# A hybrid decoder layer on one core: rows of x, one block difference, one order edge, and the opening's queues and turns moved

## The chip, the cores and the metric

The kernel runs on one core of a Trainium2 chip. The core has a matrix engine (TensorE, called PE in the profile; PEld is its weight load), a vector engine (VectorE, DVE), a scalar engine (ScalarE, ACT), GpSimd (POOL) and a queue engine (SyncE, SP) that issues most transfers. The metric is the device time of one execution in microseconds (us).

## The reference

One layer of a decoder trunk, all in float32, on x of 1024 tokens by 1024 channels:

```
h = RMSNorm(x);  [q | k | v | u | g] = h @ W_in
branch A: differential attention (8 heads, QK norm, T5 bias, causal), RMS subln, @ W_proj_attn  -> y_a
branch B: GLU(u) -> causal depthwise conv, width 31 -> LayerNorm over channels -> swish, @ W_proj_conv -> y_b
m = sigmoid(g_a) * y_a + sigmoid(g_b) * y_b
x = x + m @ W_out
x = x + (silu(gate) * up) @ W_down,   [gate | up] = RMSNorm(x) @ W_gate_up
```

## The kernel before

Every float32 matrix product is made of three reduced-precision products: each operand is split into a high part (a cast on ACT, `split_hi`) and a low part (a subtraction on DVE, `split_lo`), and PE accumulates high x high, high x low and low x high. Where two 2 x 2 block products meet, seven block products are used in place of eight (u, w_out, gate and up, w_down), which needs sums and differences of blocks beforehand.

The program is traced into a planner, which gives every instruction a place on its engine by a simulated time line, the earlier traced one first among those that are ready; `after(ins)` adds an edge that keeps the instructions traced inside it behind `ins` on the engine of `ins`. `in_order()` does that for DVE, ACT and PE at once, and `steps(...)` calls functions one after the other in that way. Each engine then runs its list strictly in order.

Four places matter here.

*The opening.* x comes in tiles of 128 rows, `xts[i]`. The first, `xts[0]`, is loaded in two halves of 512 columns on SyncE's queue. The norm weights (`anw`, two loads on ACT's queue into one partition) are spread over all partitions by a product with ones (`spread_weights`) and copied into `wb`. `squares` and `roots` give each row's factor, `norm` applies factor and weights, `turn_x` transposes on PE into banks of a pool of two (`px`, the tile name in the profile) and casts the high part, `low_x` makes the low part and so frees the bank. `keep_busy` is filler on PE. `v_tile(i, first, n)` issues `n` of the 24 matmuls by which tile i enters the first block of v. `gemm_turn` is the second product of the first half of u: four of its eight slices k (three matmuls each), then `turn_low(5)`, then the other four; after it come `turn_low(6)`, `v_tile(4)`, `turn_low(7)`, `v_tile(5)`.

*LayerNorm.* After attention, `ln_both` interleaves the two token halves of the LayerNorm (`ln_chunks`); `ln_step` advances it by a listed number of pieces between the products of `w_proj_attn`. One piece takes differences from the mean on DVE (L1573) and squares on ACT. `ya_out` multiplies a product by its gate on DVE (L1642) and stores it; `gate_of[0, 0]` is the first of these multiplications, and an `after` keeps the third `ln_step`'s DVE instructions behind it.

*The product with w_out.* Seven block products in the order of `WSEVEN`: 11, 12, S1, S2, S4, S3, 22. Each has four steps j and four row tiles i, 48 matmuls. 11 goes into the banks b, 12 into four banks a, S1 and S4 into banks c, which are the same four PSUM buffers as a; S2, S3 and 22 into b. When a block product (or its second summand) is through, four additions on DVE (L1864) take the bank into the rows of x, `xa`, and thereby free it. `wload` loads a block of w_out, `sload` loads sums of m that were stored in the stage before, `x_rows(l, c)` loads 128-row tiles of x (four for each row half l, columns of half c), and `wless(z, a, b)` makes a block difference on DVE (L1779, four instructions). All are traced at the first product, z = 0, in a written order on SyncE; the tiles `xa` lie where the stage before had its buffers.

*Weights.* `ws.next()` hands out the next pair of high and low parts and splits up to two ahead, into buffers of three.

Of the kernel before, what the change touches and what calls it, by code (L numbers as in the profile page):

```python
# [10 lines left out]
F32 = mybir.dt.float32  # L11
F32R = mybir.dt.float32r
AF = mybir.ActivationFunctionType
ALU = mybir.AluOpType
AX = mybir.AxisListType

P = 128
S = 1024
D = 1024
# [13 lines left out]
NKT = D // P  # L33
# [24 lines left out]
def kernel(  # L58
# [27 lines left out]
    nc = tc.nc  # L86
    dve, act, pool, pe = nc.vector, nc.scalar, nc.gpsimd, nc.tensor
    PSUM = bass.MemoryType.PSUM

    xs = x[0]  # L90
# [31 lines left out]
    last_lo, last_mm = [None], [None]  # L122
# [12 lines left out]
    def after(ins):  # L135

        return nullcontext() if ins is None else tc.issue_after(ins)
# [41 lines left out]
    ap = a0.enter_context(tc.tile_pool(name="a0", bufs=2, reuse_waits="tile"))  # L179
# [6 lines left out]
    xts = {}  # L186
# [3 lines left out]
        queue.dma_start(xts[i][:], xs[i * P : (i + 1) * P, :])  # L190


    anw = [ap.tile([P, 512], F32R, tag="vh", name=f"anw{g}")[0:1, :].bitcast(F32) for g in range(2)]
    one = ap.tile([1, P], F32, name="one", bufs=1)
    busy = ap.tile([P, 512], F32R, tag="vl", name="busy")
    dve.memset(f32(busy[:]), 1.0)
    dve.memset(one[:], 1.0)
    for g in range(2):
        nc.scalar.dma_start(anw[g], attn_norm_w[:, 512 * g : 512 * (g + 1)])
    xts[0] = ap.tile([P, D], F32, tag="xt", name="xt0", bufs=4)  # L200
    for g in range(2):
        nc.sync.dma_start(xts[0][:, 512 * g : 512 * (g + 1)], xs[0:P, 512 * g : 512 * (g + 1)])
    wb = ap.tile([P, D], F32, name="anw_b", bufs=1)

    def keep_busy(n):

# [138 lines left out]
    class Stream:  # L345
# [12 lines left out]
        def next(self):  # L358
            self.fetch()
            return self.have.pop(0)  # L360
# [720 lines left out]
    def opening():  # L1081
# [16 lines left out]
        def v_tile(i, first=0, n=24):  # L1098

            if i % 2 == 0 and not first:  # L1100
                o[i // 2] = pg()
            ts, dst = slice(i * P, (i + 1) * P), o[i // 2][:, 256 * (i % 2) : 256 * (i % 2 + 1)]
            order = ((0, 0), (0, 1), (1, 0)) if i else ((0, 0), (1, 0), (0, 1))
            terms = [(k, a_, b_) for a_, b_ in order for k in range(NKT)]
            for n_, (k, a_, b_) in list(enumerate(terms))[first : first + n]:
                l_, r_ = (hT_hi, hT_lo)[a_][:, k, ts], halves[k // 4][b_][:, k % 4, :]
                last_mm[0] = pe.matmul(dst, l_, r_, start=n_ == 0, stop=n_ == len(terms) - 1).ins  # L1107

        def steps(*fns):
            for fn in fns:  # L1110
                with in_order():
                    fn()
# [4 lines left out]
        def turn_low(i):  # L1117
            turn_x(i)
            low_x(i)
# [66 lines left out]
        def gemm_turn(w, mhi, mlo, sb):  # L1186

            o = pg()
            cs = slice(sb * 512, (sb + 1) * 512)

            def part(ks):
                for k in ks:
                    mm3(o[:], w[0][:, k, :], w[1][:, k, :], mhi[:, k, cs], mlo[:, k, cs], k == 0, k == NKT - 1)

            steps(lambda: part(range(4)), lambda: turn_low(5), lambda: part(range(4, NKT)))
            return o

        first_half = u_half(0, uw, 0, gemm_turn)
# [1 line left out]
        yield  # L1200
        steps(
            lambda: next(first_half),
            lambda: turn_low(6),
            lambda: v_tile(4),
            lambda: turn_low(7),
            lambda: v_tile(5),
        )
# [179 lines left out]
    steps = [(h, i) for h in range(H) for i in ORDER[h]]  # L1387
# [141 lines left out]
    part = bp.tile([P, P], F32R, tag="part", name="part", bufs=1)  # L1529
# [84 lines left out]
    def ln_step():  # L1614
        for _ in range(lnp.pop(0)):
            next(lnq, None)
# [16 lines left out]
        act.activation(g[:], g[:], AF.Sigmoid)  # L1633
        return g

    gate_of = {}

    def ya_out(c, os2, gs=None):
        for sb in range(2):
            cs = slice(sb * 512, (sb + 1) * 512)  # L1640
            g = gs[sb] if gs else gated(g_d[c], cs)
            gate_of[c, sb] = dve.tensor_tensor(g[:], os2[sb][:], g[:], op=ALU.mult).ins  # L1642
            nc.sync.dma_start(ya_d[c][:, cs], g[:])

    ln_step()
# [5 lines left out]
    first_gates = last_of(mybir.EngineType.Activation)  # L1651
# [12 lines left out]
                ln_step()  # L1664
    for c in range(NE):
        ya_out(c, o3[c], g3[c])
    with after(first_gates), after(gate_of[0, 0]):
        ln_step()
    for c in range(NE, NKT):
        with after(mean_hi if c == NE else None), after(first_gates if c == NE else None):  # L1670
# [12 lines left out]
    for cl in ((0, 1, 2), (3, 4), (5, 6), (7,)):  # L1683
        pair = [(c, ws.next()) for c in cl]
        for sb in range(2):
            cs = slice(sb * 512, (sb + 1) * 512)
            for c, w in pair:
                g = gated(g_d[NKT + c], cs)
# [79 lines left out]
    def wload(z, b_):  # L1768
        for j in range(4):
            r0 = (2 * j + b_[0]) * P  # L1770
            nc.sync.dma_start(wblock(z, j), wout[r0 : r0 + P, 512 * b_[1] : 512 * (b_[1] + 1)])
# [5 lines left out]
    def wless(z, a_, b_):  # L1777
        for j in range(4):
            dve.tensor_tensor(wblock(z, j), wblock(a_, j), wblock(b_, j), op=ALU.subtract)  # L1779

    def x_rows(l, c):
        for i in range(4 * l, 4 * l + 4):
            nc.sync.dma_start(xa[i][:, TOK[c]], xs[i * P : (i + 1) * P, TOK[c]])
# [11 lines left out]
    for z, (z_, b_, s_, (l, c), full) in enumerate(WSEVEN):  # L1795
        if z == 0:
            with after(last_of(mybir.EngineType.SP)):
                wload("12", (1, 0))
                wload("S3", (0, 1))
                wload("S1", (0, 0))  # L1800
                x_rows(0, 0)
                wload("S4", (1, 1))
                sload("S2")
                x_rows(1, 1)
                x_rows(0, 1)
                sload("S4")
                sload("S3")
                x_rows(1, 0)
        if z == 1:
            wless("S1", "S3", "S1")  # L1810
        start = s_ not in o
        if start:
            o[s_] = [p_.tile([P, 512], F32, tag=tag, name=nm("wo")) for p_, tag in wo_banks[s_]]
        for j in range(4):
            if z_ in ("S2", "S4", "S3") or j % 2 == 0:
                with after(last_of(mybir.EngineType.DVE) if z == 6 else None):
                    hi, lo = ws.next()
            if z == 1 and j == 2:
                with after(last_lo[0]):
                    wless("S2", "S4", "S1")  # L1820
            if z == 3 and j == 1:
                for q in range(2):
                    room["22", q] = wraw()[:]
                with after(last_lo[0]):
                    wless("22", "12", "S2")
                for q in range(2):
                    early_weights("22", q, 2 * q)
            if z == 4 and j == 0:
                with after(last_lo[0]):
                    wless("S3", "S4", "S3")  # L1830
            if z == 4 and j == 2:
                for q in (2, 3):
                    with after(last_lo[0]):
                        early_weights("S3", q, 2 * q)
            if z == 5 and j == 0:
                with after(last_of(mybir.EngineType.SP)):
                    for step in plain_first:
                        step.load()
            if z == 5 and j == 2:
                h2_hi = big.tile([P, NKT, S], F32R, tag="xhi", name="h2_hi")  # L1840
                h2_lo = big.tile([P, NKT, S], F32R, tag="xlo", name="h2_lo")
            for i in range(4):
                t_ = slice(i * P, (i + 1) * P)
                if z_ in ("S2", "S4", "S3"):
                    A, B = [m_[:, t_] for m_ in (hi, lo)], [m_[:, 512:] for m_ in (hi, lo)]
                else:
                    r_, k_ = {"11": (0, 0), "12": (0, 1), "22": (1, 1), "S1": (1, 0)}[z_]
                    A = [m_[2 * j + k_][:, TOK[r_]][:, t_] for m_ in (mT_hi, mT_lo)]
                    B = [m_[:, 512 * (j % 2) : 512 * (j % 2 + 1)] for m_ in (hi, lo)]
                for y_, (u_, v_) in enumerate(((0, 0), (0, 1), (1, 0))):  # L1850
                    with after(last_mm[0]), after(last_tr[0]):
                        last_mm[0] = pe.matmul(  # L1852
                            o[s_][i][:], A[u_], B[v_], start=start and j + y_ == 0, stop=j == 3 and y_ == 2,
                            skip_group_check=not start,
                        ).ins
            for t_ in NORMS.get((z, j), ()):
                with after(last_mm[0]), after(last_add if z == 6 else None), after(norm_lo if z == 6 else None):
                    norm2(t_, r2[0], tr_first)
                if z == 5:
                    norm_lo = last_lo[0]  # L1860
        for i in range(4):
            t_ = 4 * l + i
            h = xa[t_][:, TOK[c]]
            last_add = dve.tensor_tensor(h, o[s_][i][:], h, op=ALU.add).ins  # L1864
            if full:
                nc.sync.dma_start(x2_d[t_][:, TOK[c]], h)
                squares(t_, c)
        if z in (4, 6):
            r2[l] = rows_of(l)
# [267 lines left out]
```

## Time and profile before

| | us |
|---|---|
| median of 3 runs (1731.96 to 1732.47) | 1732.12 |
| the profiled execution | 1732.11 |
| its span | 1730.3 |
| PE busy | 1715.4 |
| DVE busy | 1274.0 |
| ACT busy | 863.4 |
| POOL busy | 219.0 |

The clock that the throttle granted PE was 0.999 over the span. In a row of the timeline stand the start, the duration, the engine (with a q: its queue), the line, the operation, output and inputs, shapes and count, and in brackets the idle time before it and what ended it. In the waits, the three numbers are the total, the number of times and the longest. In the chain that ended last stand start, duration and what held the end at that time.

### The profile page before, as it was taken

To read this page: it belongs to the slowest core of one execution; us is meant where nothing else is said; L and a number is where in the kernel's file an instruction comes from. 1 tells how busy PE (TensorE), PEld (TensorE's weight loads), DVE (VectorE), ACT (ScalarE), POOL (GpSimd) and SP (SyncE) were. 2 spreads that over 40 slices of the span, in tenths; PEclk is the share of its full clock that TensorE was granted. 3 is DMA by queue.
4 is the path that set the end of the run, shared out by engine and by line. 5 is a ranking of instruction groups with operands and counts; after the bars stand their busy time and mean duration, and the time that the engine had idled before them with its cause. 6 is when DMAs were issued, how large, how long until landed. Compare 5 with 4: busy or idle time off the path is not lost.

```text
span 1730.3 us, 25863 instructions
## 1 busy us (share of the span) xinstructions
PE 1715.4 (99%) x9245; PEld 1477.7 (85%) x9245; DVE 1274.0 (74%) x2128; ACT 863.4 (50%) x1958; POOL 219.0 (13%) x207
## 2 busy tenths in 40 slices
PE   9999999999999999999999999999999999999999
PEld 7997889998998998988887878888888888888887
DVE  7575889898988988877677658966676666575554
ACT  6333435767777776756566325633333333333332
POOL 3997851000000000000000000000000000000000
PEclk9999999999999999999999999999999999999999
DMA  6343445336345345353963583235455444597663
GB/s 202 117 133 121 138 150 157 104 109 173 102 129 151 108 124 151 93 147 131 332 224 123 194 302 105 74 121 171 147 166 177 154 143 157 174 362 280 215 218 131
DMA packets 261606, 281.64 MB, mean 163 GB/s; under 512 B 16547, under 2 KB 181987, under 8 KB 261477
## 3 DMA queue, kind: packets, MB, share of 16 engines
q1 hardware_dynamic: 255504, 269.55, 48.1%
q0 software_dynamic: 5680, 9.39, 2.7%
q8 instruction: 73, 1.20, 0.3%
q10 hardware_dynamic: 292, 1.05, 0.2%
q14 instruction: 57, 0.46, 0.1%
HBM read 181.84 MB, written 85.50 MB: 155 GB/s over the span
## 4 chain that ended last, share of the span: by engine, by line
PE 88%; DVE 5%; DMA 3%; ACT 2%; issue 1%; SPq 0%; ACTq 0%; DVEq 0%
PE acc L981 30%; PE acc L489 12%; PE pg L168 11%; PE pg L169 10%; PE pg L170 10%; PE wo L1852 3%; PE sc L1290 2%; PE sc L1289 2%; PE pT L1328 2%; DVE acc L595 1%; PE pW L169 1%; PE pW L168 1%; PE pW L170 1%; PE pg L1107 1%; PE pQ L816 1%
## 5 line engine op out<-in xcount | busy, mean ns | idle before, releaser
L595 DVE SCALAR_TENSOR_TENSOR acc<-u,cw,acc 128x1023 f32<-128x1023 f32 (+14 forms) x240 | 303.9, 1266 | 14.0 <-ACT acc L589 11.4
L168 PE MATMUL pg<-whi,hT_hi 128*128 128x256 f32 x704 | 199.7, 285 | 0.4 <-DVE v L125 0.4
L170 PE MATMUL pg<-whi,hT_lo 128*128 128x256 f32 x704 | 200.1, 285 | 0.0
L169 PE MATMUL pg<-wlo,hT_hi 128*128 128x256 f32 x704 | 199.4, 284 | 0.0
L125 DVE TENSOR_TENSOR wlo<-draw,whi 128x1024 fp32r<-128x1024 f32 x75 | 91.8, 1224 | 85.9 <-ACT whi L120 81.4
L120 ACT CAST whi<-draw 128x1024 fp32r<-128x1024 f32 x75 | 79.1, 1055 | 129.5 <-PE acc L489 119.3
L168 PEld LDWEIGHTS pg<-whi,hT_hi 128*128 128x128 f32 x704 | 134.0, 191 | 2.2 <-DVE v L125 0.6
L169 PEld LDWEIGHTS pg<-wlo,hT_hi 128*128 128x128 f32 x704 | 134.3, 191 | 1.8
L170 PEld LDWEIGHTS pg<-whi,hT_lo 128*128 128x128 f32 x704 | 134.2, 191 | 1.7
L120 ACT CAST whi<-wraw 128x1024 fp32r<-128x1024 f32 x90 | 94.7, 1052 | 71.0 <-PE pg L169 30.2
L489 PE MATMUL acc<-wlo,whi 128*128 128x512 f32 x308 | 119.8, 389 | 0.0
L489 PE MATMUL acc<-whi,wlo 128*128 128x512 f32 x308 | 119.8, 389 | 0.0
L1296 ACT ACTIVATE E<-E,mn 128x640 f32<-128x640 f32 (+7 forms) x128 | 99.7, 780 | 30.7 <-DVE mn L1291 29.0
L168 PE MATMUL pg<-hT_hi,whi 128*128 128x512 f32 x288 | 114.4, 397 | 0.1
L169 PE MATMUL pg<-hT_lo,whi 128*128 128x512 f32 x288 | 113.7, 395 | 0.0
L170 PE MATMUL pg<-hT_hi,wlo 128*128 128x512 f32 x288 | 113.7, 395 | 0.0
L120 ACT CAST whi<-s 128x1024 fp32r<-128x1024 f32 x54 | 56.8, 1052 | 109.0 <-PE acc L981 105.2
L125 DVE TENSOR_TENSOR wlo<-wraw,whi 128x1024 fp32r<-128x1024 f32 x75 | 92.7, 1238 | 13.7 <-ACT whi L120 13.4
L1291 DVE CUSTOM_DVE_ANT_0 E<-sc,tb 128x512 f32<-128x512 f32 (+3 forms) x128 | 74.5, 587 | 32.4 <-PE pT L1328 15.9
L981 PE MATMUL acc<-h_hi,whi 128*128 128x512 f32 x240 | 93.4, 389 | 0.0
L981 PE MATMUL acc<-h_lo,whi 128*128 128x512 f32 x240 | 93.4, 389 | 0.0
L981 PE MATMUL acc<-h_hi,wlo 128*128 128x512 f32 x240 | 90.1, 389 | 0.0
(370 smaller groups left out, 4590.5 us busy)
## 6 DMA issues: line engine op xcount, KB each, us to landing
wraw<-in_w_gate_up_dram SPq DMA_DIRECT2D x44, 512.0 KB, 4.8
wraw<-in_w_in_dram SPq DMA_DIRECT2D x40, 512.0 KB, 4.2
qs<-qs SPq DMA_DIRECT2D x96, 128.0 KB, 2.3
wd<-in_w_down_dram SPq DMA_DIRECT2D x44, 256.0 KB, 3.2
tdT<-wd SPq DMA_DIRECT2D x88, 128.0 KB, 4.8
draw<-sdS SPq DMA_DIRECT2D x44, 256.0 KB, 3.9
draw<-tdT SPq DMA_DIRECT2D x44, 256.0 KB, 3.9
wraw<-in_w_in_dram SPq DMA_DIRECT2D x32, 256.0 KB, 3.3
```

The source lines that it names most:

```text
L120: act.copy(dst, src)
L125: last_lo[0] = dve.tensor_tensor(dst, src, f32(hi), op=ALU.subtract).ins
L168: pe.matmul(o, lh, rh, start=start, stop=False)
L169: pe.matmul(o, lh, rl, start=False, stop=False)
L170: last_mm[0] = pe.matmul(o, ll, rh, start=False, stop=stop).ins
L489: m = pe.matmul(o[s_][i][:], l_[:, ts], r_[:, 512:], start=start and j + y_ == 0, stop=j == n - 1 and y_ == 2, skip_group_check=not start,)
L595: dve.scalar_tensor_tensor(a_, us[c][:, : S - n], cw[:, c, t : t + 1], a_, op0=ALU.mult, op1=ALU.add)
L981: last_mm[0] = pe.matmul(o[:], a_[x_][:, k, :], b_[y_][:, k, :], start=start and k + x_ + y_ == 0, stop=k == 3 and x_ == 1, skip_group_che ...
L1289: pe.matmul(o[:, :w], qh[:, qs], k, start=True, stop=False)
L1291: dve.tensor_tensor_reduce(e[:, ks], o[:, :w], tb[:, S - nk + c0 : S - nk + c0 + w], 1.0, mn[:, j : j + 1] if c0 else 3.0e38, ALU.add, ALU ...
L1296: act.activation(e[:, :nk], e[:, :nk], AF.Exp, bias=mn[:, j : j + 1], scale=-1.0, accum_out=l[:, j : j + 1])
L1852: last_mm[0] = pe.matmul(o[s_][i][:], A[u_], B[v_], start=start and j + y_ == 0, stop=j == 3 and y_ == 2, skip_group_check=not start,).ins
```

## The change

1. Opening: the norm weights are loaded by one transfer into row 0 of `wb` itself; the second half of `xts[0]` is issued by ACT's queue, the first by SyncE's.
2. `turn_low(5)` comes after six of the eight slices of `gemm_turn`, not four; 12 of the 24 matmuls of `v_tile(4)` come ahead of `turn_low(6)`, the other 12 behind it.
3. The edge that kept LayerNorm's differences behind the first gate multiplication is dropped.
4. In the list of loads for w_out, `x_rows(0, 0)` stands second, behind the block 12, ahead of S3 and S1.
5. The block difference S2 = S4 - S1 is traced at the start of the third product, behind the last addition of the second, and not in the middle of the second.

```
-    anw = [ap.tile([P, 512], F32R, tag="vh", name=f"anw{g}")[0:1, :].bitcast(F32) for g in range(2)]
...
-    for g in range(2):
-        nc.scalar.dma_start(anw[g], attn_norm_w[:, 512 * g : 512 * (g + 1)])
+    wb = ap.tile([P, D], F32, name="anw_b", bufs=1)
+    anw = [wb[0:1, 512 * g : 512 * (g + 1)] for g in range(2)]
+    nc.scalar.dma_start(wb[0:1, :], attn_norm_w[:, :])
     xts[0] = ap.tile([P, D], F32, tag="xt", name="xt0", bufs=4)
-    for g in range(2):
-        nc.sync.dma_start(xts[0][:, 512 * g : 512 * (g + 1)], xs[0:P, 512 * g : 512 * (g + 1)])
-    wb = ap.tile([P, D], F32, name="anw_b", bufs=1)
+    for g, queue in enumerate((nc.sync, nc.scalar)):
+        queue.dma_start(xts[0][:, 512 * g : 512 * (g + 1)], xs[0:P, 512 * g : 512 * (g + 1)])
...
-            steps(lambda: part(range(4)), lambda: turn_low(5), lambda: part(range(4, NKT)))
+            steps(lambda: part(range(6)), lambda: turn_low(5), lambda: part(range(6, NKT)))
...
             lambda: next(first_half),
+            lambda: v_tile(4, 0, 12),
             lambda: turn_low(6),
-            lambda: v_tile(4),
+            lambda: v_tile(4, 12, 12),
             lambda: turn_low(7),
...
-    gate_of = {}
-
...
-            gate_of[c, sb] = dve.tensor_tensor(g[:], os2[sb][:], g[:], op=ALU.mult).ins
+            dve.tensor_tensor(g[:], os2[sb][:], g[:], op=ALU.mult)
...
-    with after(first_gates), after(gate_of[0, 0]):
+    with after(first_gates):
         ln_step()
...
                 wload("12", (1, 0))
+                x_rows(0, 0)
                 wload("S3", (0, 1))
                 wload("S1", (0, 0))
-                x_rows(0, 0)
                 wload("S4", (1, 1))
...
             wless("S1", "S3", "S1")
+        if z == 2:
+            with after(last_add):
+                wless("S2", "S4", "S1")
...
-            if z == 1 and j == 2:
-                with after(last_lo[0]):
-                    wless("S2", "S4", "S1")
```

## The prediction

> **What bounds the kernel now.** I read the page first: which engine fills the span.
>
> ```profile
> span 1730.3 us, 25863 instructions
> ...
> PE 1715.4 (99%) x9245; PEld 1477.7 (85%) x9245; DVE 1274.0 (74%) x2128; ACT 863.4 (50%) x1958; POOL 219.0 (13%) x207
> ```
>
> TensorE (PE) is busy for 1715.4 of 1730.3 us, so only its gaps, 14.9 us in all, can be won without taking work from it, and the change takes none. The profiled execution took 1732.11 us, 1.8 us more than its span; the median of the runs is 1732.12, so I sum against 1732.1. About 0.2%, 3.46 us, is what a measurement of this kernel can tell from no change; a result below 1728.65 would count as faster.
>
> Next the waits of PE, longest first; the columns are total, times, longest.
>
> ```profile
> PE wo L1852 <- DVE xa L1864: 3.3, 2, 2.7
> ...
> PE px L725 <- DVE hT_lo L125: 1.0, 1, 1.0
> PE pg L168 <- DVE gt L1692: 0.9, 1, 0.9
> PE pg L168 <- ACT cT_hi L120: 0.8, 1, 0.8
> ...
> PE pg L168 <- DVE v L125: 0.4, 1, 0.4
> ```
>
> The first is in the product with w_out, the second in the opening where the last rows of x are turned, the third and fourth in the LayerNorm stage. These are three of the places that the change touches. I then read the timeline around each and the chain that ended last.
>
> **Product with w_out (block difference and rows of x).** Rows of the timeline, the last from the chain:
>
> ```profile
> 1011.95 3.56 SPq L1771 DMA_DIRECT2D room<-in_w_out_dram  x6
> 1015.80 1.66 SPq L1775 DMA_DIRECT2D room<-soS  x3
> 1017.82 2.28 SPq L1783 DMA_DIRECT2D xa<-in_x_dram  x4
> ...
> 1022.95 0.69 DVE L1864 TENSOR_TENSOR xa<-wo,xa 128x512 f32<-128x512 f32 x1 [3.30 <-DMA xa<-in_x_dram]
> 1023.55 1.22 DVE L125 TENSOR_TENSOR wlo<-room,whi 128x1024 fp32r<-128x1024 f32 x1
> 1024.68 2.49 DVE L1779 TENSOR_TENSOR room<-room,room 128x512 f32<-128x512 f32 x4
> 1027.10 3.07 DVE L1864 TENSOR_TENSOR xa<-wo,xa 128x512 f32<-128x512 f32 x5
> 1029.72 0.47 PE L1852 MATMUL wo<-whi,mTh 128*128 128x512 f32 x1 [2.69 <-DVE xa L1864]
> ...
> 1031.96 0.50 PE L1852 MATMUL wo<-whi,mTh 128*128 128x512 f32 x1 [0.61 <-DVE xa L1864]
> ...
> 1037.49 1.23 DVE L125 TENSOR_TENSOR wlo<-room,whi 128x1024 fp32r<-128x1024 f32 x1 [4.99 <-ACT whi L120]
> ...
> 1031.96 28.21 PE wo L1852 x123
> ```
>
> The third product, S1, starts in the banks of the second. PE had finished the second at 1029.72 - 2.69 = 1027.03. It then waited for the addition that empties its first bank. On VectorE (DVE) that addition stood behind one addition of the first product at 1022.95, a low part at 1023.55, the four S2 differences (2.49 us from 1024.68) and three more additions of the first product. The five additions from 1027.10 take 3.07 us, 0.61 each; the fourth is the one PE wanted. A second wait of 0.61 follows because S2's first low part came in between the later additions.
>
> After the change the S2 differences stand behind the last addition of the second product. Take the same landing of x's rows: first addition 1022.95 to 1023.55, low part to 1024.68 (1.13 until the next begins), three additions of 0.61 to 1026.5, the addition that PE wants to 1027.1, and with the 0.1 us that PE took after it before, PE starts at 1027.2. Each further bank is freed 0.61 later, while PE spends 3 matmuls of 28.21/123 = 0.229 us, 0.69, on each, so the second wait goes too: S2's low part can't come before its differences. Gain: 2.69 + 0.61 - 0.2 = 3.1 us.
>
> What the moved differences push: the last addition ends at 1028.9, the differences at 1031.4, S2's first low part (1.23) at 1032.7. PE wants it after 48 matmuls of S1, at 1027.2 + 48 x 0.229 = 1038.2, so 5.5 us are to spare; the cover is DVE's idle 4.99 us before 1037.49, spent waiting for a high part that waits for a buffer. Without that cover each us late is a us of PE.
>
> The rows of x moved ahead of S3's and S1's loads: cost and gain hang on what the planner makes of it. In the program x_rows(0, 0) already stands ahead of S4's four loads and of all S2 sums, and still SyncE issues it at 1017.82, behind the last six loads of w_out (which hold S4) and three of S2's sums. So its place in the program did not hold it; something it waits for did, and its space is that of gate tiles just given up, of which one is still being stored. I therefore expect the same order and no effect. The other end: the four go out second, the first product's additions are over before 1022, and the last 0.2 us go: 3.3 instead of 3.1. Then S3 and S1 come four places later; the four rows took 2.28 us to issue, so the S1 differences would end about 2.3 us later than now, at some 1021, with S1 wanted at 1027. Value taken: 3.1, ends -1.2 (worked out under the rivals) and 3.3.
>
> **Later turns.** Rows of the timeline and one of the chain:
>
> ```profile
> 34.33 2.74 DVE L715 SCALAR_TENSOR_TENSOR xt<-xt,r,anw_b 128x512 f32<-128x512 f32 x4
> 36.98 1.28 DVE L125 TENSOR_TENSOR hT_lo<-px,hT_hi 128x512 fp32r<-128x512 f32 x2
> 37.72 1.25 PE L725 MATMUL px<-ident,xt 128*128 128x128 f32 x8 [1.04 <-DVE hT_lo L125]
> 39.03 1.29 DVE L125 TENSOR_TENSOR hT_lo<-px,hT_hi 128x512 fp32r<-128x512 f32 x2 [0.77 <-ACT hT_hi L120]
> ...
> 42.61 2.88 PE pg L1107 x24
> ```
>
> PE came to turn tile 5 at 37.72 - 1.04 = 36.68, but the bank was freed by tile 4's low part only at 37.7, because DVE normalizes tiles 6 and 7 first. The change puts 18 instead of 12 matmuls ahead of the turn: 6 x 0.229 = 1.37 us more, to 38.05. The wait of 1.04 is covered with 0.3 to spare. What is late next: the turn of tile 6, wanting tile 5's low parts. These end 40.32 - 37.72 = 2.6 us after their turn begins, so at 40.65. PE has about 1.0 of turning, 6 matmuls (1.37) and 12 of v_tile(4) (24 take 2.88, so 1.44): 41.8, 1.1 us to spare. Then 12 more of v_tile(4) between tiles 6 and 7 where there were 24: about 1.0 + 1.44 = 2.4 us for banks freed in turn up to 2.6 us after the turn begins; the first is freed 0.65 earlier, and the second is wanted 0.45 later than the first. It just fits. Gain 1.04, ends 0.7 and 1.04.
>
> **Opening by two queues.** Rows of timeline and chain:
>
> ```profile
> 0.74 0.87 SPq L202 DMA_DIRECT2D xt<-in_x_dram  x2
> 1.66 1.00 SPq L1086 DMA_DIRECT2D wraw<-in_w_in_dram  x2
> 2.70 8.66 DMA xt<-in_x_dram
> ...
> 3.48 0.63 ACT L700 ACTIVATE xj<-xt 128x512 f32<-128x512 f32 x1 [1.46 <-DMA xt<-in_x_dram]
> 4.46 0.69 DVE L701 CUSTOM_DVE_ANT_0 xj<-xt 128x512 f32<-128x512 f32 x1 [2.93 <-DMA xt<-in_x_dram]
> 6.93 1.41 DVE L715 SCALAR_TENSOR_TENSOR xt<-xt,r,anw_b 128x512 f32<-128x512 f32 x2
> 8.19 1.91 PE L725 MATMUL px<-ident,xt 128*128 128x128 f32 x8
> 10.71 0.59 ACT L120 CAST hT_hi<-px 128x512 fp32r<-128x512 f32 x1
> 11.45 1.06 ACT L697 ACTIVATE xj<-xt 128x1024 f32<-128x1024 f32 x1
> ```
>
> SyncE loses one issue (0.87/2, with the gap 0.46 us); ScalarE's (ACT's) queue swaps its second norm-weight issue for x's second half, so that half is issued no earlier. w_in's first blocks and x1 go out 0.46 earlier. For: x1 landed at 2.70 + 8.66 = 11.36 and the squares began at 11.45. Against: ACT came free from the cast only at 10.71 + 0.59 = 11.30, so at most 0.1 is won. The cost: x's second half now runs beside w_in's first block instead of ahead of it. It landed 4.46 - 3.48 = 0.98 after the first half; everything to 6.93 hangs on it. The normalized half is ready about 0.7 after 6.93, and PE, busy with filler until then, turned it at 8.19: some 0.4 to 0.5 of slack. Ends: 0.1 gained and 0.55 lost (a whole 0.98 late, less 0.43); the nearest row is the slack, so I take 0.
>
> A rule of the Trainium skill speaks against this edit ("DMA: Bandwidth & Descriptors", Queues, rings and completion order): each DMA engine takes turns between the queues that have work for it, packet by packet, so the half would share with w_in's block. By that rule the opening loses up to the 0.55. No row of this profile has a half of x sharing from its start, so the trace neither bears it out nor refutes it; it is a rival below.
>
> The norm weights go into row 0 of the tile that is later overwritten: same matmuls, same copies, the halves disjoint, one issue fewer; no cost.
>
> **Norm's differences unbound.** Rows of timeline and chain:
>
> ```profile
> 843.38 0.39 PE L1567 MATMUL mean<-lnml,part 128*128 128x512 f32 x1
> 844.56 0.69 DVE L1642 TENSOR_TENSOR gt<-pg,gt 128x512 f32<-128x512 f32 x1 [3.81 <-PE pg L170]
> 846.33 0.39 PE L168 MATMUL pg<-aTh,whi 128*128 128x512 f32 x1
> ...
> 880.81 1.06 ACT whi L120
> ...
> 916.80 0.63 ACT L1633 ACTIVATE gt<-gt 128x512 f32<-128x512 f32 x1 [2.50 <-DMA gt<-g_d]
> 925.06 0.63 ACT L1633 ACTIVATE gt<-gt 128x512 f32<-128x512 f32 x1 [2.76 <-DMA gt<-g_d]
> 940.42 0.73 PE L168 MATMUL pg<-cT_hi,whi 128*128 128x512 f32 x2 [0.83 <-ACT cT_hi L120]
> ```
>
> The mean is there at about 843.8; DVE sat idle (3.81 us) until the first gate product at 844.56. The differences may now start 0.7 us earlier, one or two ahead of that product. Its bank is wanted by PE at 846.33, and the product ended at about 845.2, so one more operation of 0.6 ahead of it is hidden. Of what follows, PE's waits at 940.42 (0.83) and after (0.93) hang on a chain that starts anew from PE at 880.81 (a high part waiting for a buffer), so an earlier difference at 844 doesn't reach them; only another order in that chain could. Value 0, ends: both waits gone (1.76 gained), or four differences ahead of the product, 843.9 + 4 x 0.6 + 0.7 = 847.0 against 846.33, 0.7 lost.
>
> **Sum.** 1732.1 - 3.1 - 1.04 - 0 - 0 = 1728.0 us.
>
> **Rivals.**
> *Second half late* (two queues share): 0.55 given back, 1728.5. For: nothing keeps w_in's block behind the half any more. Against: the slack before 8.19. This is what the rule of the Trainium skill ("DMA: Bandwidth & Descriptors", Queues, rings and completion order) would make of it.
> *LayerNorm's waits go too*: 1728.0 - 1.76 = 1726.2. For: the chain behind 940.42 is order, not throughput; ACT waits in it on gate loads. Against: it restarts at 880.81.
> *The opening's gain is absorbed*: PE comes 1.04 earlier to the wait of 0.4 on v's low part, later in the projections, where DVE might be the bound: 1729.0, the same. Against: before that DVE itself waits on work that follows PE.
> *x's rows hold the queue*: SyncE stands with them till 1017.82, and S3 and S1 are issued after them, 0.59 each (3.56/6). The two blocks that S1's first step needs go out by 1020.1 + 6 x 0.59 = 1023.6 and land 5.1 later (as 1022.95 - 1017.82 shows for x's rows), at 1028.7; one difference (0.62), a high part and a low part (about 1.1 each) make 1031.5, a wait of 4.5 where there were 3.3. With the turns' gain: 1732.1 + 1.2 - 1.04 = 1732.3, the same. For: the new place in the program. Against: the planner passed them over before.
> *Slower: one more gate load enters LayerNorm's chain.* ACT works in order, and the scaling of each pair of channels stands behind a sigmoid whose load is not there yet; from one such sigmoid (916.80) to the next (925.06) are 8.26 us. If the unbinding makes the planner put one more of these ahead of the last pair, the wait at 940.42 grows by 8.26: 1728.0 + 8.26 = 1736.2. It decides as soon as that chain is over 4.1 us longer; over 7.6 it is slower beyond 0.2%. Against: PE's wait is 0.83 now, and the program order of these steps is untouched.
>
> **How the numbers follow.** Forecast 0.48, second half late 0.12 (half of it each side of 1728.65, as its cost may be less or a little more), LayerNorm 0.12, absorbed 0.12, queue held 0.05, slower 0.11. Faster: 0.48 + 0.06 + 0.12 = 0.66. Same: 0.06 + 0.12 + 0.05 = 0.23. Slower 0.11. The range goes from LayerNorm's 1726.2 to the absorbed gain with the half late beside it, 1729.0 + 0.55 = 1729.6, each rounded outward to a whole us, 1726.0 and 1730.0; it leaves out the held queue and the slower case, 0.16.
>
> **What would show it.** Right: the wait of wo on xa falls from 3.3 to 0.2 or nothing, and S2's differences stand after eight additions; no wait of px on hT_lo; PE's idle total near 10.8; the first turn still near 8.2; the wait at cT_hi near 0.8. Wrong: a wait on a low part (wlo) at the start of S1 or S2, a later x1 chain, or a longer wait on cT_hi.

## The result, and the profile after

The changed kernel took 1728.4 us (median of 20 runs, 1726.39 to 1735.99), the kernel before 1733.6 in 20 runs beside it (1731.92 to 1736.57); the ratio is 0.997, interval 0.9964 to 0.9977, so 4.0 to 6.2 us were gained where 4.1 were forecast.

The first profiled execution of the changed kernel, 1735.99 us, holds a stretch found between 60 and 80 us in no other trace of this study: two low parts took 5.83 us, PE waited 4.17 for one of them, and behind that wait the granted clock fell (1.00 up to 70 us, 0.50 from 72 to 76, 0.83 over the 20 us). Its timeline:

```profile
67.85 5.83 DVE L125 TENSOR_TENSOR wlo<-wraw,whi 128x1024 fp32r<-128x1024 f32 x2
70.41 0.39 PE L169 MATMUL pg<-wlo,hT_hi 128*128 128x256 f32 x1 [4.17 <-DVE wlo L125]
```

So I read a second profiled execution of the same kernel, 1727.72 us, that of run e5 below. Its page:

```profile
span 1726.0 us, 25866 instructions
PE 1714.5 (99%) x9245; PEld 1477.8 (86%) x9245; DVE 1275.8 (74%) x2128; ACT 861.8 (50%) x1958; POOL 218.9 (13%) x207
```

Its waits of PE (total, times, longest):

```profile
PE pm L208 <- ACT anw_b L213: 0.7, 1, 0.7
...
PE wo L1850 <- DVE xa L1862: 0.6, 1, 0.6
PE pg L168 <- DVE gt L1640: 0.5, 1, 0.5
PE pg L168 <- DVE v L125: 0.4, 1, 0.4
```

PE's idle time is 1726.0 - 1714.5 = 11.5 us, where it was 14.9. The wait of 3.3 for xa is 0.6, the 1.0 for hT_lo and the two near 940 (0.8 and 0.9) are gone; new are 0.7 behind the copies of the norm weights and 0.5 behind a gate product. The waits of the attention scores, which the change doesn't touch, make 1.6 here (1.2 for mn, 0.4 for ks) and made 0.8 before. The forecast's places, in that trace (code lines stand one or two lower than before):

```profile
1010.69 3.62 SPq L1769 DMA_DIRECT2D room<-in_w_out_dram  x6
1014.62 1.60 SPq L1773 DMA_DIRECT2D room<-soS  x3
1016.61 2.25 SPq L1781 DMA_DIRECT2D xa<-in_x_dram  x4
...
1021.81 0.69 DVE L1862 TENSOR_TENSOR xa<-wo,xa 128x512 f32<-128x512 f32 x1 [3.34 <-DMA xa<-in_x_dram]
1022.41 1.22 DVE L125 TENSOR_TENSOR wlo<-room,whi 128x1024 fp32r<-128x1024 f32 x1
1023.54 4.27 DVE L1862 TENSOR_TENSOR xa<-wo,xa 128x512 f32<-128x512 f32 x7
1026.17 0.47 PE L1850 MATMUL wo<-whi,mTh 128*128 128x512 f32 x1 [0.58 <-DVE xa L1862]
1027.73 2.49 DVE L1777 TENSOR_TENSOR room<-room,room 128x512 f32<-128x512 f32 x4
```

*w_out.* SyncE's order is that of before, six loads, three sums, then x's rows. The four differences (L1777) now follow all eight additions, and the second of the two waits is gone.

```profile
37.69 1.28 DVE L125 TENSOR_TENSOR hT_lo<-px,hT_hi 128x512 fp32r<-128x512 f32 x2
38.63 1.05 PE L724 MATMUL px<-ident,xt 128*128 128x128 f32 x8
```

*Turns.* The turn of tile 5 has no idle time ahead of it: the first low part ends at about 38.3, PE comes at 38.63.

```profile
1.31 0.36 ACTq L202 DMA_DIRECT2D xt<-in_x_dram  x1
...
5.59 0.69 DVE L700 CUSTOM_DVE_ANT_0 xj<-xt 128x512 f32<-128x512 f32 x1 [4.06 <-DMA xt<-in_x_dram]
6.78 0.20 ACT L652 ACTIVATE t<-v 128x1 f32<-128x1 f32 x1 [2.39 <-DVE v L682]
6.89 1.05 ACT L213 COPY anw_b<-pm 128x512 f32<-128x512 f32 x2
...
8.95 1.94 PE L724 MATMUL px<-ident,xt 128*128 128x128 f32 x8
```

*Opening.* x's second half is used at 5.59, not 4.46, and the first turn runs at 8.95, not 8.19: 0.76 lost. The chain that ended last shows by which way:

```profile
1.31 4.25 DMA xt<-in_x_dram
...
6.89 0.57 ACT anw_b L213
...
7.51 1.65 PE pm L208 x3
```

The half's sum of squares feeds a root on ACT (L652, at 6.78); the copies of the norm weights are queued behind that root, and the next filler on PE waits for the bank that the first copy empties. Only then comes the turn. The copy and the filler in the kernel before, where PE had no wait here:

```profile
5.76 0.57 ACT L214 COPY anw_b<-pm 128x512 f32<-128x512 f32 x1
...
6.74 1.65 PE L209 MATMUL pm<-busy 128*128 128x512 f32 x3
```

*LayerNorm.* First the new wait, then two rows of the queue and the sigmoid behind them. The last two rows are gate products (L1690) of the loop that follows LayerNorm; it multiplies the products of w_proj_conv by their gates and adds y_a, and I call it the merge loop.

```profile
846.68 2.48 DVE L1640 TENSOR_TENSOR gt<-pg,gt 128x512 f32<-128x512 f32 x4
847.42 0.50 PE L168 MATMUL pg<-aTh,whi 128*128 128x512 f32 x1 [0.46 <-DVE gt L1640]
...
919.80 0.32 SPq L1632 DMA_DIRECT2D gt<-g_d  x1
920.97 0.38 SPq L301 DMA_DIRECT2D wraw<-in_w_proj_conv_dram  x1
922.81 0.63 ACT L1633 ACTIVATE gt<-gt 128x512 f32<-128x512 f32 x1
...
940.63 0.68 DVE L1690 TENSOR_TENSOR gt<-pg,gt 128x512 f32<-128x512 f32 x1
943.13 1.29 DVE L1690 TENSOR_TENSOR gt<-pg,gt 128x512 f32<-128x512 f32 x2 [1.81 <-PE pg L170]
```

The same places in the kernel before, the third row from the chain that ended last:

```profile
920.36 0.38 SPq L302 DMA_DIRECT2D wraw<-in_w_proj_conv_dram  x1
920.84 0.53 SPq L1632 DMA_DIRECT2D gt<-g_d  x1
...
920.84 4.20 DMA gt<-g_d
...
943.39 1.89 DVE L1692 TENSOR_TENSOR gt<-pg,gt 128x512 f32<-128x512 f32 x3 [1.43 <-PE pg L170]
944.73 0.50 PE L168 MATMUL pg<-cT_hi,whi 128*128 128x512 f32 x1 [0.93 <-DVE gt L1692]
```

The four differences from the mean now start at 844.28 and run ahead of the gate product at 846.68; before, they came behind that product, which ran at 844.56. Further on, the last gate load stood before on SyncE behind a block of weights that waited for its buffer; its sigmoid came at 925.06 after an idle 2.76, and the chain that ended last went through that load. Now the load is ahead of that block, and the sigmoid runs at 922.81 without a wait. And of the merge loop's gate products, one now runs at 940.63, ahead of the two that wait for PE; before, three ran in a row at 943.39.

### The profile page after: what moved, and what is told of

Same layout as the page of the kernel before. It is cut to its first block, busy times and chain, and to the rows that moved or that the text cites. A ratio compares the mean times of both kernels' runs of the same rounds, so it can differ in the third digit from the quotient of the medians.

```text
span 1734.2 us, 25866 instructions
## 1 busy us (share of the span) xinstructions
PE 1718.1 (99%) x9245; PEld 1480.7 (85%) x9245; DVE 1286.8 (74%) x2128; ACT 862.0 (50%) x1958; POOL 219.1 (13%) x207
## 3 DMA queue, kind: packets, MB, share of 16 engines
q10 hardware_dynamic: 434, 1.32, 0.2%
## 4 chain that ended last, share of the span: by engine, by line
PE 94%; DVE 3%; DMA 2%; ACT 1%; issue 1%; SPq 0%; DVEq 0%; ACTq 0%
PE acc L980 30%; PE acc L488 12%; PE pg L168 12%; PE pg L169 12%; PE pg L170 12%; PE wo L1850 4%; PE sc L1289 2%; PE sc L1290 2%; PE pT L1328 2%; DVE acc L594 1%; PE pg L1106 1%; PE pW L168 1%; PE pW L169 1%; PE pW L170 1%; PE pQ L815 1%
```

## The experiments

| run | what it is | median us (runs) | ratio to the kernel before, interval |
|---|---|---|---|
| e1 | without part 1 | 1726.08 (5) | 0.9957, 0.9945 to 0.997 |
| e2 | part 5 alone | 1729.59 (11) | 0.9979, 0.997 to 0.9988 |
| e3 | part 2 alone | 1731.78 (11) | 0.9993, 0.9984 to 1.0002 |
| e4 | part 3 alone | 1731.89 (11) | 0.9992, 0.9983 to 1.0001 |
| e5 | all parts again | 1727.72 (5) | 0.9968, 0.9955 to 0.998 |
| e6 | all, half alone on its queue | 1727.23 (5) | 0.9965, 0.9951 to 0.9978 |
| e7 | all, halves on one queue | 1727.35 (5) | 0.9964, 0.9951 to 0.9976 |
| e8 | as e1, fourth difference behind | 1726.84 (5) | 0.9963, 0.995 to 0.9975 |
| e9 | before, products in order | 1732.39 (11) | 0.9993, 0.9984 to 1.0001 |
| e10 | as e1, two differences behind | 1728.47 (7) | 0.997, 0.9959 to 0.9981 |
| e11 | as e8, products in order | 1725.19 (5) | 0.9952, 0.9939 to 0.9964 |
| e12 | part 1 alone | 1734.22 (11) | 1.0003, 0.9994 to 1.0012 |

The kernel before had medians of 1733.32 (e1 to e4), 1733.61 (e5 to e8) and 1734.14 (e9 to e12). An interval is 2 to 4 us wide, so single effects under 1 us are read from the traces.

**e1, without the opening.** The diff is that of the change without its first two hunks (`anw`, `xts[0]`).

> The changed kernel with the opening of before (both halves of x's first tile on SyncE's queue, two loads of norm weights). Theory: the second half on ACT's queue shares the DMA engines with w_in's first block and lands about 1.1 us later, which costs PE 0.7 us; so this kernel's first turn is back at 8.2 us, PE waits 0.6 less, and it is 0.7 us faster than the changed kernel, 5.5 to 6 faster than before (about 1727.5 where before has 1733). Rival, the late half belongs to the one disturbed execution that was profiled: no difference to the changed kernel, 5 us faster than before.

The median was the lowest of its batch. By the ratios it is 2.2 us below the changed kernel, where 0.7 was expected, but the intervals overlap, so the time doesn't size the effect. In the trace the turn is back at 8.19, and the new wait of 0.46 behind the gate product is there, so that wait isn't the opening's.

**e2, the block difference alone.**

```
+        if z == 2:
+            with after(last_add):
+                wless("S2", "S4", "S1")
...
-            if z == 1 and j == 2:
-                with after(last_lo[0]):
-                    wless("S2", "S4", "S1")
```

> Before, with only S2's block difference moved behind the additions of the second product. Theory: both waits of PE for xa (2.7 and 0.6) go, at most 0.2 is left, the rows of x are issued where they were: 3.1 to 3.3 us faster than before. Rival, the place of x's rows does the work: little or no gain here, PE's wait stays near 2.5.

```profile
1029.25 0.47 PE L1852 MATMUL wo<-whi,mTh 128*128 128x512 f32 x1 [0.56 <-DVE xa L1864]
```

One wait of 0.56 is left of two that made 3.3, where at most 0.2 was expected; it is the same as with x's rows moved too (0.58). With SyncE's order unchanged as well, the move of x's rows did nothing. Of the single parts only this one is faster beyond its interval.

**e3, the turns alone.** The diff is the hunk with `range(6)` and that with `v_tile(4, 0, 12)`.

> Before, with only the later turns of tiles 5 and 6. Theory: PE's wait of 1.0 for tile 4's low part goes and nothing later takes it back: 1.0 us faster. Rival, the gain is absorbed by the wait on v's low part (0.4 in before, would be 1.4) or in LayerNorm: no gain.

PE's wait of 1.0 for hT_lo is gone from the list of waits, and those near 940 (0.83 and 0.92) and on v's low part (0.4) stand; on xa there is one of 3.1 in place of two that made 3.3 (the last section comes back to it); the time fell by 1.2 of 1733.3 by the ratio, which the interval does not tell from nothing.

**e4, the edge alone.**

```
-    with after(first_gates), after(gate_of[0, 0]):
+    with after(first_gates):
```

> Before, with only the edge dropped that held LayerNorm's differences behind the first gate product. Theory: the planner's other order removes PE's waits of 0.8 and 0.9 near 940 us and puts one of 0.5 on the gate product near 845: about 1.2 us faster. Rival, those waits went through the shift of everything before: they stay here, and the time is as before or 0.5 slower.

Both waits near 940 are gone and the one of 0.46 near 847 is new: 1.76 - 0.46 = 1.3 in the trace; the ratio makes it 1.4, no more certain than for the turns. In this kernel too the gate load is issued ahead of the block (919.33 and 920.58). So it is this edge, far upstream, that moved the gate load and the product.

**e5, all parts again.** Same kernel as the changed one.

> The changed kernel once more, for a second profile of it. Theory A: what the opening by two queues costs sits before 16 us: x's second half lands near 5.5 us (4.44 before) and the first turn runs near 8.9 (8.19 before), and everything after it is about 0.7 later; the median should be 0.5 to 1.0 above that of the kernel of this batch that keeps only the single load of the norm weights. Rival B: the stretched instructions between 64 and 74 us in the first profile belong to the changed kernel: they come back, a wait of PE of some 4 us with them, and the span is 4 to 5 us above. Rival C: the opening costs nothing that lasts, being taken up by the later wait on v's low part: medians within 0.3 of each other.

The stretch between 60 and 80 us did not come back. The opening behaves as in the first profile (5.54 and 8.90 there). Against e7 the median is only 0.37 higher, within the intervals.

**e6, the second half alone on its queue.**

```
-            nc.sync.dma_start(
+            nc.scalar.dma_start(
                 raw[:].rearrange("p (k c) -> p k c", c=256),
...
-        xload(1)
+        xload(1, nc.scalar)
```

> All parts of the change, and besides w_in's first two blocks and x's second tile are issued on ScalarE's queue, behind x's second half, instead of on SyncE's; so nothing but x's first half runs beside the second half. Theory A (the half is late because it shares the DMA engines with w_in's first block): it lands at 4.3 to 4.6 instead of 5.5, the first turn is back near 8.2, and the kernel is 0.5 to 0.8 below all parts. Rival B (ScalarE's queue or its later issue is what is slow): the half still lands at 5.3 or later and the first turn stays near 8.9. Rival C: w_in's blocks, issued some 0.6 later, become what is late: the half lands early, and a wait on wraw or on the first high part of w_in replaces it, no gain.

```profile
1.32 0.36 ACTq L202 DMA_DIRECT2D xt<-in_x_dram  x1
4.83 0.69 DVE L700 CUSTOM_DVE_ANT_0 xj<-xt 128x512 f32<-128x512 f32 x1 [3.30 <-DMA xt<-in_x_dram]
8.20 1.94 PE L724 MATMUL px<-ident,xt 128*128 128x128 f32 x8
```

Issued by the same queue at the same time as in e5 (1.32 and 1.31), the half is used 0.76 earlier and the turn runs 0.75 earlier (the half was expected at 4.3 to 4.6, a little earlier still). The queue isn't slow; what ran beside the half was w_in's blocks. The packets in the traces show it: while the half's 256 KB moved, from 3.3 to 5.2 us in e5, SyncE's queue began 402 KB of w_in's packets; here, from 2.5 to 4.5, 180 KB of other packets began. This agrees with the rule of the Trainium skill ("DMA: Bandwidth & Descriptors", Queues, rings and completion order) that a DMA engine takes turns between the queues that have work. The median is in the interval of e5's.

**e7, one load of the norm weights, both halves on SyncE.**

```
-    for g, queue in enumerate((nc.sync, nc.scalar)):
-        queue.dma_start(xts[0][:, 512 * g : 512 * (g + 1)], xs[0:P, 512 * g : 512 * (g + 1)])
+    for g in range(2):
+        nc.sync.dma_start(xts[0][:, 512 * g : 512 * (g + 1)], xs[0:P, 512 * g : 512 * (g + 1)])
```

> All parts of the change but one: both halves of x's first tile are issued on SyncE as before; the norm weights still come by one load into the tile's first row. Theory A: that load costs and gains nothing: the second half lands near 4.4, the first turn near 8.2, time as without the whole opening part (1726.1), 0.5 to 1.0 below all parts. Rival B (the norm weights' one load is what is late): the first filler of the broadcast runs later and the first turn stays near 8.9.

```profile
4.79 0.69 DVE L700 CUSTOM_DVE_ANT_0 xj<-xt 128x512 f32<-128x512 f32 x1 [3.27 <-DMA xt<-in_x_dram]
8.19 1.91 PE L724 MATMUL px<-ident,xt 128*128 128x128 f32 x8
```

The turn is back at 8.19: the single load costs nothing in the trace, the second queue is the whole loss.

**e8, the fourth difference behind the gate product.** On e1, with `gate_of` kept as before:

```
-            dve.tensor_tensor(d[:], cc[c], mean[:], op=ALU.subtract)
+            with after(gate_of[0, 0] if sb == 0 and c == 3 else None):
+                dve.tensor_tensor(d[:], cc[c], mean[:], op=ALU.subtract)
```

> All parts but the opening, and of LayerNorm's first four differences the last is bound behind the first gate product again, so that three go ahead of that product. By the order written down, the gate load that matters in the chain before the second half of LayerNorm still goes out ahead of the weight block (behind it in the kernel before). Theory A: the wait of 0.46 near 847 (a bank's gate product behind four differences) goes, as the product comes 0.6 earlier; and the two waits that stood at 940 and 944 stay away, because they hang on that one load standing behind a weight block that waits for its buffer; 0.4 to 0.5 below the kernel with one norm load. Rival B (they stayed away because the differences as a whole began earlier): with a difference behind the product again, some of the 0.83 and 0.93 return, and no gain.

```profile
844.36 0.68 DVE L1644 TENSOR_TENSOR gt<-pg,gt 128x512 f32<-128x512 f32 x1
...
916.75 0.32 SPq L1634 DMA_DIRECT2D gt<-g_d  x1
917.86 0.38 SPq L302 DMA_DIRECT2D wraw<-in_w_proj_conv_dram  x1
...
940.79 1.89 DVE L1694 TENSOR_TENSOR gt<-pg,gt 128x512 f32<-128x512 f32 x3 [3.21 <-PE pg L170]
942.14 0.50 PE L168 MATMUL pg<-cT_hi,whi 128*128 128x512 f32 x1 [0.93 <-DVE gt L1694]
```

My theory was half wrong; by time, 0.5 below e7, within the intervals. The wait near 847 went and the first one near 940 stayed away, with the gate load ahead of the block. But the second, 0.93, was back, and three products run in a row again: it has a cause of its own. In VectorE's list the product of the first channel's second half stands ahead of that of its first half, which had long been ready; PE wants the latter's bank.

**e9, the products in order, on the kernel before.**

```
-    M = {}
+    M, mul = {}, {}
...
-                dve.tensor_tensor(g[:], o[:], g[:], op=ALU.mult)
+                with after(mul[0, 0] if (c, sb) == (0, 1) else None):
+                    mul[c, sb] = dve.tensor_tensor(g[:], o[:], g[:], op=ALU.mult).ins
```

> The kernel before with one edge added: the third product of the merge loop (first channel, second half of the rows) may stand on VectorE only behind the first (same channel, first half). Orders of TensorE and of SyncE stay those of before. Theory A (the wait of 0.93 at 944.73 comes from the finished product of the first half standing behind one whose matmuls are still running): that wait goes, the one of 0.83 at 940.42 stays; 0.9 faster than before. Rival B (both waits come from the late chain of the scaling): both stay and the time is that of before.

```profile
940.29 0.73 PE L168 MATMUL pg<-cT_hi,whi 128*128 128x512 f32 x2 [0.43 <-ACT cT_hi L120]
```

The wait of 0.93 is gone, the one on cT_hi is left. So the second wait is the products' order. (The first is 0.43 here and 0.4 to 1.0 in all six profiles with the old order of the queue; none of the eight with the new order has it.) By time, 1.2 faster, not certain.

**e10, two differences behind.** As e8, with `c == 2`.

> All parts but the opening; of LayerNorm's first four differences the third and fourth stand behind the first gate product again. By the order written down the last gate load of the chain is issued behind the weight block again, as in the kernel before, and the merge loop's first product stands behind the third, as in the kernel before. Theory A (the gate load's place decides the wait of 0.83, the product's place that of 0.93): the wait of 0.46 near 847 stays away, and both waits near 940 are back, 1.7 to 1.8 in all; about 0.8 slower than the run with the fourth difference alone behind. Rival B (the earlier start of two differences is enough): no wait near 940, fastest of this batch but one.

```profile
918.98 0.38 SPq L302 DMA_DIRECT2D wraw<-in_w_proj_conv_dram  x1
919.45 0.53 SPq L1634 DMA_DIRECT2D gt<-g_d  x1
...
938.77 0.73 PE L168 MATMUL pg<-cT_hi,whi 128*128 128x512 f32 x2 [0.60 <-ACT cT_hi L120]
943.09 0.50 PE L168 MATMUL pg<-cT_hi,whi 128*128 128x512 f32 x1 [0.93 <-DVE gt L1694]
```

One difference more behind the product, and the block is ahead of the gate load again; both waits are back, 0.60 and 0.93. The ratio is 1.2 us above e8's, where 0.8 was expected; the intervals overlap. That settles the rival: the differences' earlier start does not help by itself; the first wait goes with the queue's order, the second with the products'.

**e11, three waits gone.** e8's and e9's edits together, on e1.

> All parts but the opening, the fourth difference behind the first gate product, and the edge that puts the merge loop's products in order. Theory A: neither the wait of 0.46 near 847 nor those of 0.83 and 0.93 near 940; against the kernel without the opening (1726.1 in its batch) 0.46 less, against the kernel before 3.3 + 1.0 + 1.76 = 6.1 less, less what the w_out stage still waits (0.5): ratio 0.9965 to 0.996. Rival B: PE, coming earlier, meets the next weight block or bank, and a new wait of 0.5 to 1 stands behind 945.

```profile
PE wo L1855 <- DVE xa L1867: 0.9, 1, 0.9
```

None of the three waits is in its list, and the wait on xa grew to 0.9: PE arrives 3.46 after the first addition, against 3.78 in e5. So some of what was won upstream is lost there, much as the rival had it. The ratio is better than the expected 0.996, by more than these waits explain (the spells told of in the last section may be part of it). At 1725.19 it is the fastest kernel here; its interval, 0.9939 to 0.9964, ends where that of the change begins.

**e12, the opening alone.**

> The kernel before with the opening by two queues and one load of the norm weights, nothing else. Theory A: x's second half lands near 5.5, the first turn runs near 8.95 instead of 8.19, and the 0.76 stays to the end: 0.5 to 1.0 slower than before. Rival B: later waits of the projections take it up, and the time is that of before to within 0.2.

```profile
6.27 0.69 DVE L700 CUSTOM_DVE_ANT_0 xj<-xt 128x512 f32<-128x512 f32 x1 [4.74 <-DMA xt<-in_x_dram]
9.64 0.66 PE L724 MATMUL px<-ident,xt 128*128 128x128 f32 x2
```

Half and turn are later still in this execution, because the first half landed late too (used at 4.92). The time is 0.5 above before by the ratio, between 1.0 below and 2.1 above: a loss of 0.76 fits, none fits too. How far the loss lasts can be followed in the traces: at the turn of tile 4 (33.63 in e5, 32.83 in e2), and up to the wait on v's low part, which ends at 300.7 in e12 and at 299.3 in the kernel before. At 798 the two traces are within 0.1 us of each other; e12 has none of the attention scores' waits, where the kernel before has 0.8, and the rest of the recovery I can't place. So to the end the loss isn't shown.

## Why the prediction came out right

By the profiles, before to e5: -2.7 (w_out), -1.0 (turns), -1.3 (LayerNorm), +0.76 (opening) make -4.2. The forecast was -3.1, -1.04, 0 and 0. The total was right by luck: what LayerNorm gave, 1.3, is about what the opening (0.76) and w_out (0.4) fell short. That the spans differ by nearly the same, 1726.0 - 1730.3 = -4.3, is partly chance too: PE's idle time fell by 3.4 only (14.9 to 11.5), because the attention scores' waits were 0.8 longer in e5, and PE's busy time is 0.9 shorter, for which I have no cause. Of the signs named beforehand, the place of the differences and the turns came true; idle was 11.5, not 10.8, the first turn was at 8.95, not 8.2, and the wait at cT_hi was gone.

- *w_out, 3.1: right mechanism, 0.4 too much.* PE started S1 4.36 after the first addition (1026.17 - 1021.81), forecast 4.25. But PE arrived 3.78 after it, not 4.08: x's rows landed 0.3 nearer to PE's arrival, which leaves 0.58 in place of 0.2. The wait goes with that distance; it is nothing to 0.9 in the traces with the edit.
- *x's rows moved, no effect: right.* SyncE's order stayed; the rival that had them hold the queue is out.
- *Turns, 1.04 with 0.3 to spare: right* (38.63 against 38.3). The rival that had the gain absorbed is out: the wait on v's low part is 0.4 before and after.
- *Opening, 0: wrong.* "Second half late" came true, larger than its bound of 0.55. The half was 1.13 late, not at most 0.98; and the slack that I named was that of the normalized half, while PE was held by ACT's copies, queued behind the root. The first copy ended at 6.33 before and PE came to the filler at 6.74, a slack of 0.41; it ended at 7.46 after, 1.13 later. I costed the late half on one path and did not list what stands behind the waiting instruction on ACT. In e4, with before's opening, the half happened to be used at 5.01, 0.55 later than before, and the turn came at 8.38, 0.19 later: a half later by more than that slack reaches PE there too.
- *LayerNorm, 0: wrong.* Both bounds happened. The four differences do stand ahead of the product and cost 0.46 (bound 0.7); both later waits went (1.76). My reason against it, that the chain starts anew at 880.81, speaks of time handed down, not of the planner's order, which the edge changed 70 us downstream; I had named that order as the one way and not followed it. The slower rival was the same place with the other sign: a gate load out of the way, not one more in it.
- *The level.* The sum started from 1732.1; before's later medians are 1.2 to 2.0 above that, 1733.6 beside the changed kernel. The gain measured there is 5.2 (4.0 to 6.2), so the forecast of 1728.0 met 1728.4 partly because gain and level were both low, by 1.1 and 1.5. What the gain has beyond the traces' 4.2 lies within the interval; the spells of low clock in the last section may be part of it.

## What to carry to other kernels

Follow a late operand along every engine that waits for it, and list what is queued behind the waiting instruction there: the loss came through a copy that does not use the operand. Where an order is planned from dependencies, dropping an edge moves transfers and products far downstream; compare each queue's order near the later waits before calling them out of reach. And look at what is issued beside two halves of a first tile before putting them on two queues: here a transfer that used to stand behind the half then shared with it and the turn came at 8.95, and with less beside it (e6) the turn was at 8.20, no earlier than the 8.19 of one queue.

## What had not been expected of the hardware

The first transfers land at different times in different executions: x's second half, with both halves on one queue, was used between 4.19 and 5.01 in ten traces, and in e12 even the first half came at 4.92 where the others had 3.48 to 3.70. The waits of the attention scores on ks, qs and mn varied too, none to 2.1 us in total per trace, in kernels that do not differ there; single profiles settle waits, not totals. What stretched the low parts of the first execution between 60 and 80 us was not found.

The granted clock also fell behind long waits of PE. In e3, e4 and e12, which keep the old place of the block difference, it was 0.69 and 0.73 from 1026 to 1030 us (e3, e4) and 0.68 from 1030 to 1034 (e12), just behind the waits on xa, of which the longest is 2.8 to 3.1. In e4 the first seven of S1's matmuls take 3.06 us, most of them 0.43 apart, where the usual 0.23 makes some 1.7. Each bank's addition then comes in time, and e3 and e4 have one wait on xa and not two; that the slower pace is the reason fits, but no run tests it. The kernel before and e9 waited 2.7 and 2.8 at the same place without such a spell, and none of the nine traces with the difference moved has one there. So the old order may have cost more than its waits in some executions, and the prediction's sum has no term for it. No run isolates what it is worth.
